# Rotation tables a layer early, joins spread over the blocks, two phase planes and a later turn in a two-model kernel

## The chip, the cores and the metric

The kernel runs on one core of a Trainium2 chip. The metric is the device time of one execution in microseconds (us), the median of several runs. PE is the matrix engine, DVE the vector engine, ACT the scalar engine, POOL is GpSimd, SP the engine that only issues DMAs.

## The reference

Two models run one after the other on one sequence of 256 rows with 1024 features, in float32.

```python
def first_block(x, mem, ...):
    for l in range(2):
        h = rmsnorm(x, g[0])
        y = even_mixer(...) if l % 2 == 0 else odd_mixer(...)   # pooling + gated recurrence / banded attention
        x = x + rmsnorm(y, g[1])
        x = x + rmsnorm(memory_cross_attention(rmsnorm(x, g[2]), mem_n, ...), g[3])
        x = x + rmsnorm(squared_relu_mlp(rmsnorm(x, g[4]), w_ff1[l], w_ff2[l]), g[5])

def second_block(x, ...):
    h = x + diff_attention(rms_norm(x, n0), w_qkv, q_gain, k_gain, lam_vecs, subln, w_o, lam, cos, sin)
    h = h + squared_relu_mlp_2(rms_norm(h, m0), w_up[0], w_down[0])
    h = h + s5_layer(rms_norm(h, n1), a, log_dt, b, c, d_skip, w_glu)     # diagonal state space, both directions
    return h + squared_relu_mlp_2(rms_norm(h, m1), w_up[1], w_down[1])
```

`diff_attention` normalizes each head of q and k, multiplies by a gain and rotates the head by `cos` and `sin`; its two softmax maps are subtracted with a factor made from `lam_vecs`. `s5_layer` is a linear recurrence over 256 steps in 64 groups of 16 features.

## The kernel before, in words

**Layout.** The running value `X` lies as two row tiles of 128 rows (t = 0 and 1). Each float32 operand of a matmul is held as two reduced-precision parts (hi and lo), so every product is three matmuls. A weight comes by a 512 KB load on SP's queue into `raw` (four buffers); ACT rounds it into `whi` (L53, L47), DVE makes `wlo` (L58, L49). Ten `whi` and ten `wlo` tiles form a ring.

**Order.** A list scheduler puts the instructions of each engine in order. Every engine and every DMA queue then works in that order. `manual_schedule(engines=...)` keeps the order of the code for some engines, `low(...)` lowers the priority of what is made inside it.

**Residual.** `residual(t, acc, ...)` normalizes a projection's result and adds it to `X`: DVE `y` (L187), ACT square, DVE `r` (L170), POOL power (L171), DVE `r` (L194) and two `X` (L200). Then PE turns the row tile (tp, L140), and ACT and DVE (L144) make its hi and lo features for the next projection. `row_scale(t)` makes the row factor of the next norm by the same square, `r` and power; the square is ACT's `junk<-X` (L168).

**End of the first model.** At the start of its second MLP, `reorder` writes `X` to DRAM (`d_x`) and reads it back in another row order. That MLP (`perm`) needs `row_scale` of the reordered `X` only at its end, for the residual. Next comes `diff`, which loads cos, sin, the gains and `lam_vecs` and makes the rotation tables (L661 to L674: 17 small DVE operations, one ACT exponential) before the q and k projections.

**Tables of the state-space layer.** While the second MLP of the first model and the first MLP of the second run, the generator `tables` fills in work for blocks 0 to 7 and 8 to 15. Per block POOL makes complex products (`cmt`, L1165 and L1166) that DVE's `gr` and `er` use, and POOL issues DMAs of `gr`, `eo` and `kl` to DRAM (`d_g`, `d_e`, `d_kl`). After the eighth block of a half, POOL joins the eight `kl` of the half in DRAM (two DMAs d_ks<-d_kl, L1450 and L1451), and then issues eight DMAs d_tt<-d_ks (L1456) that re-lay them. The layer loads `e`, `t` (from `d_tt`) and `g` on SP's queue.

**State-space layer.** `ssm` begins when the MLP's residual is done: 48 scaled copies `xp` (L1522 on DVE, L1524 on ACT, L1526 on POOL; two loops over t, the first over both halves h at once, the second half by half), then PE turns them (utp, L1538), multiplies with `e` (zt), rotates phases with the planes of `tbs` (cos, sin, minus sin; two buffers), and makes the outputs from `t` and `g` (yp). `h` (L1610, L1611) are DVE's products with the planes.

**Even mixer.** Its last step normalizes the recurrence's output `y` (L1124), PE turns it (otp, L1127), ACT and DVE make features from it, and the projection `w_out` follows.

## Time and profile before

| | |
|---|---|
| three runs, median (lowest to highest) | 1492.5 us (1489.15 to 1496.48) |
| the profiled execution | 1488.93 us, span of its core 1487.2 us |
| PE busy | 1414.7 us, 95% of the span |
| DVE, ACT, POOL busy | 1103.8, 859.4, 234.4 us |
| mean granted clock of PE | 0.985 of full speed |

PE is busy nearly all the time, so what it waits for is the difference between its 1414.7 us and the span: some 72 us in all, in places that the view of waits names. A change of another engine's work counts where such a place hangs on it.

### The profile page before, as it was taken

How to read it: one execution, taken by the hardware profiler on the slowest of the kernel's cores; microseconds unless marked ns; L12 is line 12 of the kernel's file. 1: busy time of each engine (PE TensorE's matmuls, PEld its weight loads, DVE VectorE, ACT ScalarE, POOL GpSimd, SP SyncE). 2: the span in 40 equal slices, each digit the busy share in tenths (PEclk: the TensorE clock that was granted, in tenths of full speed). 3: DMA queues.
4: the chain of work that ended last, by engine and by line, in shares of the span. 5: the costliest groups of instructions: out<-in, count | busy, mean ns of one | idle time of the engine just before them, and what ended most of it. 6: DMA issues, size and time to landing. Idle time of an engine off the chain costs nothing.

```text
span 1487.2 us, 25549 instructions
## 1 busy us (share of the span) xinstructions
PE 1414.7 (95%) x9668; PEld 1231.5 (83%) x9668; DVE 1103.8 (74%) x1965; ACT 859.4 (58%) x1480; POOL 234.4 (16%) x290
## 2 busy tenths in 40 slices
PE   8899999999999999999999789999999878999997
PEld 8897888998889798878888667888889666889895
DVE  7996658997676866569998589889995487665651
ACT  7475547565564665566656557667656463554540
POOL 1232001000010000014634210033551200000000
PEclk9999999999999999999999999999999998999999
DMA  8465535475875356366677734357779977455640
GB/s 302 143 198 170 185 125 177 157 257 193 287 256 184 119 180 200 112 207 207 220 242 265 254 124 142 100 161 241 238 236 334 346 280 262 153 187 180 210 159 29
DMA packets 121236, 298.26 MB, mean 201 GB/s; under 512 B 15129, under 2 KB 24121, under 8 KB 120473
## 3 DMA queue, kind: packets, MB, share of 16 engines
q1 hardware_dynamic: 113848, 271.40, 55.3%
q0 software_dynamic: 7264, 25.24, 4.6%
q8 instruction: 76, 1.25, 0.3%
q14 instruction: 48, 0.39, 0.1%
HBM read 270.15 MB, written 31.62 MB: 203 GB/s over the span
## 4 chain that ended last, share of the span: by engine, by line
PE 73%; DVE 13%; DMA 6%; issue 4%; ACT 3%; POOL 1%; SPq 0%; DVEq 0%; ACTq 0%; POOLq 0%
PE ffacc L217 7%; PE ffacc L219 7%; PE ffacc L218 7%; PE ffps L224 5%; PE ffps L226 5%; PE ffps L225 5%; PE pacc L219 4%; PE pacc L218 4%; PE pacc L217 4%; DVE wlo L58 3%; PE pb L225 3%; PE pb L224 3%; PE pb L226 3%; DMA raw<-in_w_ff 2%; PE ffps L219 2%
## 5 line engine op out<-in xcount | busy, mean ns | idle before, releaser
L58 DVE SCALAR_TENSOR_TENSOR wlo<-raw,gcols,whi 128x512 fp32r<-128x512 f32 (+1 forms) x456 | 356.7, 826 | 75.6 <-ACT whi L53 75.3
L53 ACT ACTIVATE whi<-raw,gcols 128x512 fp32r<-128x512 f32 (+1 forms) x456 | 317.0, 745 | 104.4 <-PE pb L226 17.3
L47 ACT ACTIVATE whi<-raw 128x1024 fp32r<-128x1024 f32 x176 | 182.8, 1055 | 155.6 <-DMA raw<-in_w_ff 59.3
L49 DVE TENSOR_TENSOR wlo<-raw,whi 128x1024 fp32r<-128x1024 f32 x172 | 210.1, 1241 | 84.1 <-ACT whi L47 80.1
L224 PE MATMUL ffps<-hh,whi 128*128 128x256 f32 x768 | 220.2, 287 | 2.7 <-ACT eo L1419 1.5
L226 PE MATMUL ffps<-hl,whi 128*128 128x256 f32 x768 | 218.2, 284 | 0.0
L225 PE MATMUL ffps<-hh,wlo 128*128 128x256 f32 x768 | 217.6, 283 | 0.0
L217 PE MATMUL ffacc<-whi,ah 128*128 128x512 f32 x512 | 204.7, 400 | 0.0
L219 PE MATMUL ffacc<-whi,al 128*128 128x512 f32 x512 | 202.2, 395 | 0.0
L218 PE MATMUL ffacc<-wlo,ah 128*128 128x512 f32 x512 | 202.1, 395 | 0.0
L224 PEld LDWEIGHTS ffps<-hh,whi 128*128 128x128 f32 x768 | 146.0, 190 | 5.3 <-ACT eo L1419 2.0
L225 PEld LDWEIGHTS ffps<-hh,wlo 128*128 128x128 f32 x768 | 145.7, 190 | 0.6
L226 PEld LDWEIGHTS ffps<-hl,whi 128*128 128x128 f32 x768 | 145.8, 190 | 0.0
L219 PEld LDWEIGHTS ffacc<-whi,al 128*128 128x128 f32 x512 | 96.4, 188 | 22.7
L217 PEld LDWEIGHTS ffacc<-whi,ah 128*128 128x128 f32 x512 | 96.5, 188 | 22.5 <-issue 1.8
L218 PEld LDWEIGHTS ffacc<-wlo,ah 128*128 128x128 f32 x512 | 96.5, 189 | 20.8
L225 PE MATMUL pb<-hh,wlo 128*128 128x256 f32 x352 | 101.2, 289 | 2.6 <-DVE wlo L58 2.6
L224 PE MATMUL pb<-hh,whi 128*128 128x256 f32 x352 | 101.2, 290 | 2.2 <-ACT whi L53 2.2
L226 PE MATMUL pb<-hl,whi 128*128 128x256 f32 x352 | 100.8, 287 | 0.0
L171 POOL TENSOR_TENSOR r<-r,mhalf 128x1 f32<-128x1 f32 x32 | 23.3, 730 | 463.9 <-DVE r L170 457.4
L303 ACT ACTIVATE relu<-ffps 128x512 f32<-128x512 f32 x64 | 43.8, 685 | 54.9 <-PE ffps L226 36.4
L225 PEld LDWEIGHTS pb<-hh,wlo 128*128 128x128 f32 x352 | 68.4, 195 | 3.4 <-DVE wlo L58 3.3
(488 smaller groups left out, 3024.9 us busy)
## 6 DMA issues: line engine op xcount, KB each, us to landing
raw<-in_w_ff SPq DMA_DIRECT2D x128, 512.0 KB, 4.6
raw<-in_ffn_w_up SPq DMA_DIRECT2D x64, 512.0 KB, 4.7
raw<-in_ffn_w_down SPq DMA_DIRECT2D x64, 512.0 KB, 4.6
raw<-in_w_mem_kv SPq DMA_DIRECT2D x32, 512.0 KB, 4.7
raw<-in_w_qkv SPq DMA_DIRECT2D x24, 512.0 KB, 4.7
raw<-in_attn_w_qkv SPq DMA_DIRECT2D x24, 512.0 KB, 5.0
raw<-in_w_in_ab SPq DMA_DIRECT2D x20, 512.0 KB, 6.5
raw<-in_w_mem_q SPq DMA_DIRECT2D x16, 512.0 KB, 4.6
```

The lines of the kernel that those rows point to most:

```text
L47: nc.scalar.activation(out=hi, in_=src, func=AF.Copy)
L49: eng.tensor_tensor(out=lo, in0=src, in1=hi.bitcast(F32), op=ALU.subtract)
L53: nc.scalar.activation(out=hi[:, a], in_=src[:, a], func=AF.Copy, scale=g)
L58: nc.vector.scalar_tensor_tensor(out=lo[:, a], in0=src[:, a], scalar=g, in1=hi[:, a].bitcast(F32), op0=ALU.mult, op1=ALU.subtract)
L171: nc.gpsimd.tensor_tensor(out=r, in0=r, in1=self.mhalf[:, 0:1], op=ALU.pow)
L217: nc.tensor.matmul(o, xh, wh[:, s], start=first, stop=False)
L218: nc.tensor.matmul(o, xh, wl[:, s], start=False, stop=False)
L219: nc.tensor.matmul(o, xl, wh[:, s], start=False, stop=last)
L224: nc.tensor.matmul(out, wh, xh, start=first, stop=False)
L225: nc.tensor.matmul(out, wl, xh, start=False, stop=False)
L226: nc.tensor.matmul(out, wh, xl, start=False, stop=last)
L303: nc.scalar.activation(out=o, in_=ps if view is None else ps.rearrange("p (f c j) -> p f c j", f=2, j=8), func=AF.Relu)
```

## The change

1. The rotation tables move from `diff` to a method `rotations`, called ahead of the MLP that stands before `diff`, with low priority and buffers of their own.
2. `row_scale` of the reordered rows is pinned on ACT behind the output of chunk 3 of that MLP.
3. The joins are made block by block: `join(k - 1)` is issued on POOL's queue in block k. Only the eighth block's join and the eight re-layouts (`step_tables`) come after a half. Those of the first half are pinned on POOL behind the first `prep` of `diff`, those of the second half behind POOL's `xp`; `d_tt` is two tensors.
4. The phase planes are two, not three: minus sin is made by a factor (`nsgn`, or -1.0), and `h1` is two operations. `tbs` has three buffers. POOL's order around `xp` is that of the code.
5. The even mixer's last step for t = 0 and 1 is queued as `features` and taken inside the projection `w_out` (at row tile 1, k tile 2 at the latest); `y` of t = 1 gets a buffer of its own.

```diff
@@ mlp: scales, and the loop over chunks
             for t in range(2):
-                if perm:
-                    self.row_scale(t)
...
-            parts[ch] = out_b(ps)
+            if perm and ch == 3:
+                with self.tc.manual_schedule(engines={nc.scalar.engine}):
+                    parts[ch] = out_b(ps)
+                    for t in range(2):
+                        self.row_scale(t)
+            else:
+                parts[ch] = out_b(ps)
@@ diff
-    def diff(self, pool, w_qkv, gain, q_gain, k_gain, lam_vecs, subln, w_o, cos2, sin2, done):
+    def rotations(self, pool, q_gain, k_gain, lam_vecs, subln, cos2, sin2):
...
-        def rotations():
+        with self.low(600):
...
+        self.tabs, self.sg, self.nlam = tabs, sg, nlam
+
+    def diff(self, pool, w_qkv, gain, w_o, done):
...
-        rotations()
...
-        k0 = prep(0, a, "k", put_k[0])
+        with self.tc.manual_schedule(engines={nc.gpsimd.engine}):
+            k0 = prep(0, a, "k", put_k[0])
+            self.step_tables(0)
@@ even
-            y = self.sb.tile([128, 4, 128], F32, tag="y", name="y")
+            y = pool.tile([128, 4, 128], F32, tag="t2", name="y") if t else self.sb.tile([128, 4, 128], F32, tag="y", name="y")
...
+            self.later.append(features)
+        self.proj_a(hh, hl, w_out, 0, done, turns=HALF, share=True, now=(1, 2))
@@ tables
-                    tb = pool.tile([128, 3, 16, 32], F32, tag="pre_tb", name="tb")
+                    tb = pool.tile([128, 2, 16, 32], F32, tag="pre_tb", name="tb")
-                    V.tensor_scalar(out=tb[:, 2], in0=s1, scalar1=sgn, scalar2=-1.0, op0=MU, op1=MU)
...
+                    if g2 == 0 and k > blocks[0]:
+                        self.join(k - 1)
...
-            nc.gpsimd.dma_start(out=ks[a0:a1, :, :, 112:240], in_=kl5[a0:a1, :, 0, :, 0:128])
-            nc.gpsimd.dma_start(out=ks[a0:a1, :, :, 0:112], in_=kl5[a0:a1, :, 1, :, 32:144])
-            for r in range(8):
-                nc.gpsimd.dma_start(out=self.d_tt[r * 16:r * 16 + 16, 4 * a0:4 * a1, :], in_=src)
+    def join(self, k):
+        self.nc.gpsimd.dma_start(out=ks[:, :, 112:240], in_=kl[:, 0, :, 0:128])
+        self.nc.gpsimd.dma_start(out=ks[:, :, 0:112], in_=kl[:, 1, :, 32:144])
+    def step_tables(self, half):
+        self.join(8 * half + 7)
+        for r in range(8):
+            self.nc.gpsimd.dma_start(out=self.d_tt[half][r * 16:r * 16 + 16], in_=src)
@@ load_phases, ssm
-        t = self.pre.tile([128, 3, 16, 32], F32, tag="tbs", name="tbs", bufs=2)
+        t = self.pre.tile([128, 2, 16, 32], F32, tag="tbs", name="tbs", bufs=3)
...
+        with self.tc.manual_schedule(engines={G.engine}):
+            for t in range(2):
...
+            self.step_tables(1)
...
-            V.tensor_tensor(out=h1, in0=sr, in1=tbs[:, 1:3], op=MU)
+            V.tensor_tensor(out=h1[:, 0], in0=sr[:, 0], in1=tbs[:, 1], op=MU)
+            V.scalar_tensor_tensor(out=h1[:, 1], in0=sr[:, 1], scalar=-1.0, in1=tbs[:, 1], op0=MU, op1=MU)
@@ first model, layer 1
+        if l == 1:
+            c.rotations(c.rot_pool.__enter__(), ...)
```

Line numbers in the rows below are those of each kernel's own file; in the changed one the rotations are L664 to L677, DVE's `xp` is L1544, `cmt` is L1178 and L1179, the joins are L1467 and L1468, d_tt is L1475, d_g is L1420, d_e is L1432 and d_kl is L1448.

The first place is DVE at the end of the first model's second MLP, where ffacc_7392 and ffacc_7393 (before) hold the MLP's result for row tile 0, and 7394 and 7395 that for row tile 1. Before:

```order
L187 TENSOR_TENSOR y<-ffacc_7392,gB 128x512
L187 TENSOR_TENSOR y<-ffacc_7393,gB 128x512
L170 TENSOR_SCALAR r<-ms 128x1
L58 SCALAR_TENSOR_TENSOR wlo<-raw,gcols,whi 128x512 x16
L661 TENSOR_SCALAR qkg<-qkg 128x64
...
L669 TENSOR_TENSOR lp<-lv 128x128
L671 TENSOR_REDUCE ls<-lp 128x2
L673 TENSOR_TENSOR nlam<-ls 128x1
L674 TENSOR_SCALAR nlam<-nlam 128x1
L194 TENSOR_TENSOR r<-r,rsq 128x1
L200 SCALAR_TENSOR_TENSOR X<-y,r,X 128x512 x2
L187 TENSOR_TENSOR y<-ffacc_7394,gB 128x512
```

The same place in the changed kernel, where 7430 and 7431 are row tile 0 and 7432 and 7433 row tile 1:

```order
L187 TENSOR_TENSOR y<-ffacc_7430,gB 128x512
L187 TENSOR_TENSOR y<-ffacc_7431,gB 128x512
L170 TENSOR_SCALAR r<-ms 128x1
L194 TENSOR_TENSOR r<-r,rsq 128x1
L200 SCALAR_TENSOR_TENSOR X<-y,r,X 128x512 x2
L58 SCALAR_TENSOR_TENSOR wlo<-raw,gcols,whi 128x512 x3
L170 TENSOR_SCALAR r<-ms 128x1
L58 SCALAR_TENSOR_TENSOR wlo<-raw,gcols,whi 128x512 x3
L144 TENSOR_TENSOR hl<-tp,hh 128x512 x2
L58 SCALAR_TENSOR_TENSOR wlo<-raw,gcols,whi 128x512 x4
L187 TENSOR_TENSOR y<-ffacc_7432,gB 128x512
L187 TENSOR_TENSOR y<-ffacc_7433,gB 128x512
```

The residual of row tile 0 (L194, L200) now stands right behind its L170; sixteen `wlo` and the tables stood between. On PE the eight turns `tp` of row tile 0 stood behind the last matmul of the MLP; before:

```order
L217 MATMUL ffacc_7395<-whi,ah 128x512
L218 MATMUL ffacc_7395<-wlo,ah 128x512
L219 MATMUL ffacc_7395<-whi,al 128x512
L140 MATMUL tp<-ident,X 128x128 x8
L217 MATMUL acc_9369<-whi,hh 128x512
```

In the changed kernel they stand 24 matmuls ahead of the MLP's end, in this piece:

```order
L217 MATMUL ffacc_7433<-whi,ah 128x512
L218 MATMUL ffacc_7433<-wlo,ah 128x512
L219 MATMUL ffacc_7433<-whi,al 128x512
L140 MATMUL tp<-ident,X 128x128 x8
L217 MATMUL ffacc_7432<-whi,ah 128x512
```

So the MLP's last 24 matmuls, and then 21 of the next projection (`acc`), now stand between the turns of row tile 0 and the first of row tile 1.

The second place is DVE at the start of the state-space layer, where ffacc_11129 to 11132 (before) hold the MLP's result, two tiles for each row tile. Before:

```order
L200 SCALAR_TENSOR_TENSOR X<-ffacc_11129,rsq,X 128x512
L200 SCALAR_TENSOR_TENSOR X<-ffacc_11130,rsq,X 128x512
L170 TENSOR_SCALAR r<-ms 128x1
L49 TENSOR_TENSOR wlo<-raw,whi 128x1024 x2
L200 SCALAR_TENSOR_TENSOR X<-ffacc_11131,rsq,X 128x512
L200 SCALAR_TENSOR_TENSOR X<-ffacc_11132,rsq,X 128x512
L170 TENSOR_SCALAR r<-ms 128x1
L1522 TENSOR_SCALAR xp<-X,r 32x16x16 x11
L1522 TENSOR_SCALAR xp<-X,r 32x8x16 x22
```

In the changed kernel:

```order
L200 SCALAR_TENSOR_TENSOR X<-ffacc_11151,rsq,X 128x512
L170 TENSOR_SCALAR r<-ms 128x1
L1544 TENSOR_SCALAR xp<-X,r 32x16x16 x11
L49 TENSOR_TENSOR wlo<-raw,whi 128x1024 x2
L200 SCALAR_TENSOR_TENSOR X<-ffacc_11152,rsq,X 128x512
L200 SCALAR_TENSOR_TENSOR X<-ffacc_11153,rsq,X 128x512
L1527 TENSOR_SCALAR nsgn<-sgn 128x1
L170 TENSOR_SCALAR r<-ms 128x1
L1544 TENSOR_SCALAR xp<-X,r 32x8x16 x22
```

The eleven copies of row tile 0 stand ahead of the residual of row tile 1. The third place is POOL in the middle of a half, in one block of `tables`; `d_kl` is that block's last DMA. Before:

```order
L1434 DMA d_kl<-kl 128x144
L1408 DMA d_g<-gr 128x1024
L1165 TENSOR_TENSOR cmt<-pk,bb 128x512
L1166 TENSOR_TENSOR cmt_8773<-pk,bb 128x512
L1420 DMA d_e<-eo 128x512 x2
```

In the changed kernel:

```order
L1448 DMA d_kl<-kl 128x144
L1420 DMA d_g<-gr 128x1024
L1467 DMA d_ks<-d_kl 64x1x128
L1468 DMA d_ks<-d_kl 64x1x112
L1432 DMA d_e<-eo 128x512 x2
L1178 TENSOR_TENSOR cmt<-pk,bb 128x512
L1179 TENSOR_TENSOR cmt_8824<-pk,bb 128x512
```

The join, which must wait until `d_kl` has landed, now stands ahead of the products that DVE needs for the next block; this is so, or nearly so, in fourteen blocks.

## Rows read from the trace of the kernel before

**Rows 1.** Waits of PE: waited for, us in total, times, longest.

```profile
PE tp L140 <- issue: 11.1, 1, 11.1
PE utp L1538 <- DVE xp L1522: 9.2, 1, 9.2
...
PE yp L1617 <- DMA g<-d_g: 4.0, 3, 2.1
...
PE fftp L345 <- ACT relu L307: 3.1, 1, 3.1
PE otp L1127 <- DVE y L1124: 2.7, 2, 2.0
```

**Rows 2.** PE's timeline around the MLP's end: start, us, instruction, idle before.

```profile
845.71 0.40 PE L217 MATMUL ffacc<-whi,ah 128*128 128x512 f32 x1
...
846.88 0.40 PE L219 MATMUL ffacc<-whi,al 128*128 128x512 f32 x1
858.36 1.94 PE L140 MATMUL tp<-ident,X 128*128 128x128 f32 x8 [11.09 <-issue]
```

**Rows 3.** DVE's timeline, same place.

```profile
837.69 0.21 DVE L170 TENSOR_SCALAR r<-ms 128x1 f32<-128x1 f32 x1 [0.85 <-ACT junk L168]
...
846.94 5.43 DVE L58 SCALAR_TENSOR_TENSOR wlo<-raw,gcols,whi 128x512 fp32r<-128x512 f32 x8 [3.03 <-ACT whi L53]
853.23 0.20 DVE L661 TENSOR_SCALAR qkg<-qkg 128x64 f32<-128x64 f32 x1 [0.87 <-DMA qkg<-in_attn_q_gain]
...
857.51 1.41 DVE L200 SCALAR_TENSOR_TENSOR X<-y,r,X 128x512 f32<-128x512 f32 x2
858.96 1.29 DVE L187 TENSOR_TENSOR y<-ffacc,gB 128x512 f32<-128x512 f32 x2
...
863.10 1.42 DVE L200 SCALAR_TENSOR_TENSOR X<-y,r,X 128x512 f32<-128x512 f32 x2
```

**Rows 4.** POOL's timeline ahead of it.

```profile
830.73 0.66 POOL L1450 DMA_DIRECT2D d_ks<-d_kl  x1 [5.07 <-DMA d_kl<-kl]
...
834.22 5.09 POOL L1456 DMA_DIRECT2D d_tt<-d_ks  x8 [2.19 <-DMA d_ks<-d_kl]
839.38 0.77 POOL L171 TENSOR_TENSOR r<-r,mhalf 128x1 f32<-128x1 f32 x1
```

**Rows 5.** Windows: us; PE, PEld, DVE, ACT, POOL busy (instructions); PE clock; DMA share; GB/s.

```profile
666.00:671.00 5.00, 4.67 (x27) 4.67 (x28) 5.00 (x6) 3.94 (x7) 3.64 (x3) 0.67 0.64 211
...
700.00:850.00 150.00, 141.94 (x1040) 122.92 (x1038) 125.46 (x186) 93.90 (x156) 65.22 (x78) 1.00 0.75 248
...
858.00:870.00 12.00, 11.64 (x50) 9.51 (x51) 7.20 (x16) 8.11 (x20) 1.65 (x3) 0.82 0.11 40
870.00:940.00 70.00, 65.94 (x344) 53.19 (x343) 67.45 (x150) 46.51 (x89) 6.40 (x3) 1.00 0.45 143
...
1185.00:1197.00 12.00, 4.20 (x59) 3.59 (x62) 10.23 (x34) 7.05 (x17) 4.00 (x9) 0.57 1.03 412
```

**Rows 6.** ACT's timeline where the perm MLP's row factor waits.

```profile
659.70 0.64 ACT L168 ACTIVATE junk<-X 128x512 f32<-128x512 f32 x1 [6.47 <-DMA X<-d_x]
```

**Rows 7.** DVE's timeline at the state-space layer's start, then PE's.

```profile
1182.94 1.45 DVE L200 SCALAR_TENSOR_TENSOR X<-ffacc,rsq,X 128x512 f32<-128x512 f32 x2 [4.90 <-PE ffacc L219]
...
1185.31 10.59 DVE L1522 TENSOR_SCALAR xp<-X,r 32x256 f32<-32x256 f32 x33
...
1192.81 1.94 PE L1538 MATMUL utp<-ident,xp 128*128 128x128 f32 x8 [9.20 <-DVE xp L1522]
```

**Rows 8.** Waits of SP's queue: the loads of the phase planes.

```profile
SPq L1494 <- DVE h L1611: 7.2, 2, 6.5
```

**Rows 9.** One block's product: POOL's timeline, then DVE's.

```profile
789.40 1.39 POOL L1165 TENSOR_TENSOR cmt<-pk,bb 128x512 f32<-128x512 f32 x1 [3.09 <-issue]
...
792.73 0.68 DVE L1169 TENSOR_TENSOR er<-er,cmt 128x512 f32<-128x512 f32 x1
```

**Rows 10.** POOL's groups: busy us, mean ns of one, idle before.

```profile
L1420 POOL DMA_DIRECT2D d_e<-eo x32 | 17.9, 561 | 53.6 <-ACT eo L1419 49.3 <-DVE wlo L49 3.0 <-DMA pk<-d_p 1.3
```

## What the change will do to the time, forecast from the trace

> **What bounds the kernel.** PE works nearly all the time, so I began with the view of what PE waited for [rows 1]. Five of its waits touch the change: 11.1 us for the turns `tp` behind the first model's last MLP, 9.2 us for the turns `utp` of the state-space layer, 4.0 us for `g`, 3.1 us in the reordered MLP and 2.7 us in the even mixer. Next came the timelines around each, to see what ends last there, and then windows, to see which engine binds after it.
>
> The largest is put down to nothing ("issue"). PE's last MLP matmul starts at 846.88 and the turns at 858.36 [rows 2]. DVE's timeline tells why [rows 3]: the residual of row tile 0 had its `r` at 837.69, but in DVE's order sixteen `wlo` (one wait of 3.03 us for ACT among them) and the rotation tables from 853.23 came first, and its two `X` ran at 857.51. POOL's power for it was held too, behind the eight re-layouts, until 839.38 [rows 4]. Afterwards the granted clock averages 0.82 over 858 to 870, a mixture of the lower level (1.2 GHz) just after the idle stretch and the full one, and from 870 to 940 DVE is busy 67.45 of 70 us [rows 5]: there DVE binds, not PE.
>
> **A, the MLP's end.** The tables leave this place and the residual of row tile 0 stands right behind its `r`. The re-layouts are no longer ahead of POOL's power, so with 0.21 for `r`, 0.77 for the power [rows 4], as much as `r` again for the small product and 1.41 for two `X` [rows 3] the row tile is ready at about 837.7 + 2.6 = 840.3. The turns are now placed 24 matmuls before the MLP's end. Matmuls start (846.88 - 845.71) / 5 = 0.234 us apart [rows 2], so that place is at 847.3 - 5.6 = 841.7, and the turns come 1.4 us after their data. The 11.1 us go, and the clock's loss with them, (1 - 0.82) x 12 = 2.2 us [rows 5]: 13.3 us at most. New is the chain of row tile 1. Behind the MLP's last matmul stand 21 matmuls of the projection, 4.9 us. The chain from its `y` to its last `X` took 858.96 to 864.52, 5.6 us [rows 3]; four `wlo` of 0.68 us stand inside it now, in part in its own waits: 5.6 to 8.3 us. PE thus waits 0.7 to 3.4 us; I take 2.0, so A is -11.3 us. The lower bound: if DVE binds from 838 on, only its relief counts, the tables with their waits, from 853.23 to the `X` at 857.51, 4.3 us. I stay near the upper end because DVE is busy only 7.20 of the 12 us from 858 to 870 [rows 5], room for the `wlo` that now come later.
>
> **Where the tables go.** 17 small operations, their six loads and one exponential move into the MLP before, ahead of DVE's first `al`. DVE is not full there, and PE has two chunks in hand: 0.
>
> **B, the row factor.** ACT waited 6.47 us for the reordered `X` [rows 6] with the next chunk's `relu` behind it, and PE waited 3.1 us for that [rows 1], then ran from 666 to 671 at 0.67 of the clock, (1 - 0.67) x 5 = 1.65 us [rows 5]. The factor is used only at the MLP's end. Pinned behind chunk 3 it finds `X` landed: -4.75 at best. In the new order of SP's queue one weight load and the small loads of the first block stand behind the reordered `X`, and DVE's products of these stand ahead of two `wlo`; none is needed before chunk 2 is through, some 20 us later. I take -4.5; bounds 0 and -4.75.
>
> **C, the even mixer.** PE has the projection's matmuls to do while DVE makes `y`; 36 of them are 8.4 us against waits of 2.7 us [rows 1]: -2.5, bounds 0 and -2.7.
>
> **D, the state-space layer's start.** `utp` starts 7.5 us after DVE's first copy; the eleven copies left by then run until 1195.9, 3.1 us [rows 7]. So 22 had to be done. In the new order the eleven large ones of row tile 0 run in the 4.90 us in which DVE waits for PE [rows 7], and eleven small ones, 3.1 us, are left ahead of `utp`: 7.5 - 3.1 = -4.4. A gap of about 4.8 us stays, and so does the low clock (0.57 from 1185 to 1197 [rows 5]). The bound on the other side is 0, if `e`, not `xp`, sets the pace.
>
> **E, planes and the second re-layout.** SP's queue stood 7.2 us for the planes' buffers with loads of `g` behind it [rows 8]; a third buffer ends that. PE's waits for `g` are 4.0 us in all [rows 1], and `g` needs ring slots besides: -1.2, bounds 0 and -4.0. `h1` in two operations adds less than one of 0.68 us [rows 9] in each of four blocks while PE waits for other things: 0, at worst +2.7. Against it, eight re-layouts, 2 MB, move from a stretch where PE never waits into one whose DMA share is already 1.03 [rows 5]. The first half took 8.6 us from join to last issue [rows 4]. Behind POOL's 4.0 us of `xp` [rows 5] this ends near 1185.3 + 4.0 + 8.6 = 1198; the `t` that needs it is loaded later, behind a load that waits for a buffer. What it slows is `e`: I take +1.5, bounds 0 and +6.
>
> **F, the joins.** 28 more DMA issues of 0.66 us [rows 4] are 18 us on POOL, 1.3 us in each of 14 blocks, and each join can wait up to 5.07 us for its `kl` to land [rows 4]. Behind it wait `d_e`, then the next product. DVE takes that product 792.73 - 790.79 = 1.9 us after POOL made it [rows 9]. A join with its wait uses this up; but POOL is busy 65 of 150 us and DVE 125 [rows 5], and `wlo` are made ahead. I take +1.5 us in all, bounds 0 and +14 (1 us a block).
>
> **Sum.** -11.3 - 4.5 - 2.5 - 4.4 - 1.2 + 1.5 + 1.5 = -20.9. The profiled execution took 1488.9 us, so its like would take 1468.0. The median of the runs, 1492.5, is 3.6 above it, so I forecast 1471 (1468.0 + 3.6, rounded down). About 0.5%, 7.5 us, is what a measurement of this kernel can tell from no change: faster is below 1485, slower above 1500.
>
> **Rival 1: DVE takes the place of the wait.** From 870 DVE has 2.5 us to spare in 70 [rows 5]. If the `wlo` that now come later hold the projection back, A gives the 4.3 us of the tables alone, 7.0 less: -13.9, 1479. For it speaks DVE's full stage, against it the idle 4.8 us just ahead. Chance 0.17.
>
> **Rival 2: the second re-layout starves the layer.** If the 2 MB delay `e` and `t` by what they need at the DMA's full load, +6 and the gain of D's 4.4 given back in part (3.0): -20.9 + 4.5 + 3.0 = -13.4, 1479. For it the DMA share of 1.03, against it that the queue keeps this `t` behind everything that is needed earlier. Chance 0.12.
>
> **Rival 3: the joins hold POOL, POOL holds DVE, DVE holds PE.** One mechanism, its place in each of 14 blocks: join ahead of product. A full wait of 5.07 plus 1.3 less the margin of 1.9 is 4.5 us a block, 63 us: -22.4 + 63, 1533. It decides at 7.5 + 22.4 = 29.9 us, 2.1 us a block passed on to PE; from 1.1 us a block on the whole change is within 0.5%, about 1490. Against it: `d_g` often stands between `d_kl` and the join, PE waited for none of these products before, and DVE has slack. Chance 0.05 slower, 0.10 within 0.5%. The longer an issue takes, the likelier this is; a `d_e` issue took 0.561 us on average over 32, all in stretches where DVE was busy [rows 10]. The Trainium skill, "SBUF — State Buffer", in "A bandwidth-pool intuition that's wrong (but worth ruling out)", says that a DMA issued by GpSimd is held while DVE runs a copy in a two-port mode, some 3100 ns instead of 620; by that 28 issues would cost 87 us of POOL, not 18, and this rival would be the likeliest. The 32 issues show no such hold, so its chance stays small.
>
> **Chances and range.** The forecast itself has 0.56 (1464 to 1476, its own range), rivals 1 and 2 have 0.29, also faster; so faster 0.85, within 0.5% 0.10, slower 0.05. The range reaches down to A's and E's best ends without the two costs (-2.0 - 2.8 - 3.0, 1463.6) and some more, 1460, and up through rivals 1 and 2 to 1486.
>
> **What would show it.** A: the turns of row tile 0 lie inside the MLP's matmuls without idle time, row tile 1's wait at most 3.4 us, the clock near full. B: no wait at `fftp`. C: none at `otp`. D: `utp` waits about 4.8 us. E: fewer waits for `g`; `zt` waits more for `e`. F: POOL's wait for `d_kl` in many blocks, but DVE's waits for `cmt` small. Wrong it would be if DVE waits for `cmt` in many blocks, if a `wlo` is late where the tables stood, or if `X` of row tile 0 comes after 841.7 by that clock and stops the MLP itself.

## The result, and the profile after

| | median us (lowest to highest, runs) | profiled execution: time, span |
|---|---|---|
| before | 1490.42 (1488.81 to 1496.48, 5) | 1488.93, 1487.2 |
| after | 1504.56 (1502.31 to 1507.65, 5) | 1503.47, 1501.7 |

The median of before stands here for the five runs beside those of after. The ratio is 1.0091, 95% interval 1.0064 to 1.0119: 14 us slower, where 21 us faster was forecast. No rival gave this time either; the third had the right sign and put it on the joins, but by a mechanism that, as will be seen, the largest wait does not show. One run of f1 was slow (1564.78 us, at a granted clock of 0.842) and is left out of the median of f1 below.

Waits of PE in the profile of after (waited for, us in total, times, longest); the first five answer to [rows 1].

```profile
PE tp L140 <- issue: 1.6, 1, 1.6
PE utp L1561 <- DVE xp L1544: 6.2, 1, 6.2
PE yp L1641 <- DMA g<-d_g: 1.3, 1, 1.3
PE fftp L345 <- ACT relu L307: 1.1, 1, 1.1
PE otp L1138 <- DVE y L1133: 0.5, 1, 0.5
...
PE ffps L224 <- ACT eo L1431: 6.9, 2, 5.9
PE ytp L1664 <- DVE wt L1655: 5.7, 2, 3.9
PE tq L750 <- DVE z L744: 5.4, 2, 3.4
...
PE ffps L225 <- DVE wlo L58: 4.2, 2, 3.5
...
PE ffps L224 <- DVE al L298: 2.1, 1, 2.1
```

All five waits that the prediction aimed at became shorter, by 19.4 us together (11.1 + 9.2 + 4.0 + 3.1 + 2.7 against 10.7), and others took their place. Where, the start times of the same PE instructions tell, read in both traces:

| stretch, by the clock of before | after minus before, us |
|---|---|
| to the reordered MLP (638), with the even mixer (C) | -2.7 |
| 638 to 666, the turns `fftp` (B) | -3.2 |
| 666 to 727 | +6.8 |
| 727 to 847, the MLP's last matmul | +8.5 |
| 847 to 860, the turns behind it (A) | -13.1 |
| 860 to 986, the differential attention | +15.5 |
| 986 to 1181, the next MLP, with the second fill (F) | +2.1 |
| 1181 to 1193, the turns `utp` (D) | -3.0 |
| 1193 to the end (E) | +3.6 |
| sum, as the spans differ | +14.5 |

Each trace is of one execution. At 638 the kernels run below that hold the same edit of the mixer stand between 3.2 us ahead of before and 1.6 us behind it, so a stretch tells differences of 2 or 3 us only where several traces agree.

A went as forecast, which PE's timeline shows where [rows 2] had 11.09 us; the same view has the largest new wait and one in the attention.

```profile
812.55 0.58 PE L224 MATMUL ffps<-hh,whi 128*128 128x256 f32 x1 [5.90 <-ACT eo L1431]
...
863.03 0.63 PE L140 MATMUL tp<-ident,X 128*128 128x128 f32 x4 [1.58 <-issue]
...
944.35 1.97 PE L750 MATMUL tq<-ident,z 128*128 128x128 f32 x8 [3.42 <-DVE z L744]
```

Three places pay for it. **First, the attention.** Windows of after (columns as in [rows 5]):

```profile
858.00:870.00 12.00, 10.35 (x48) 7.90 (x47) 9.11 (x18) 9.66 (x21) 1.54 (x2) 1.00 0.61 192
...
920.00:940.00 20.00, 20.00 (x89) 16.18 (x88) 14.20 (x24) 12.85 (x15) 0.00 (x0) 1.00 0.55 184
940.00:960.00 20.00, 14.74 (x92) 12.33 (x91) 16.84 (x29) 7.42 (x13) 2.06 (x2) 0.83 0.33 106
```

The clock just behind the MLP is full now (1.00 where it was 0.82 [rows 5]), so A's clock term came too. But from 940 to 960 PE is busy 14.74 of 20 us and the clock 0.83: PE has run out of other work. Its order says why. The attention has 288 projection matmuls (`acc`) to put between the turns and scores; how many stand ahead of a group of turns `tq`, or of the second half's scores, was counted in the PE order of each trace:

```
projection matmuls ahead of:             third tq group   second half's first 24 scores
before                                        221                 265
after                                         288                 288
run g1 (below), re-layout not pinned          221                 265
run x2 (below), joins together                211                 288
```

In after all of them are used up before the second key half's `tq`, and nothing is left to cover the chain of turns, scores and softmax behind it. DVE's timeline there:

```profile
937.95 2.69 DVE L58 SCALAR_TENSOR_TENSOR wlo<-raw,sg,whi 128x1024 fp32r<-128x1024 f32 x2 [2.19 <-ACT whi L53]
940.55 1.41 DVE L58 SCALAR_TENSOR_TENSOR wlo<-raw,gcols,whi 128x512 fp32r<-128x512 f32 x2
941.88 1.22 DVE L742 TENSOR_TENSOR z<-z,y 128x1024 f32<-128x1024 f32 x1
...
943.61 1.28 DVE L744 TENSOR_TENSOR z<-z,r 128x512 f32<-128x512 f32 x2
```

And POOL's, with the pinned block of ten issues behind its first `y`:

```profile
874.84 0.68 POOL L1467 DMA_DIRECT2D d_ks<-d_kl  x1
...
878.48 5.00 POOL L1475 DMA_DIRECT2D d_tt<-d_ks  x8 [2.31 <-issue]
897.10 2.39 POOL L739 TENSOR_TENSOR y<-kc,ta 128x1024 f32<-128x1024 f32 x1 [13.63 <-ACT kc L714]
```

POOL is not late: its second `y` is done at 899.5, 42 us before DVE's `z` that uses it (941.88), and POOL waited 13.6 us for ACT ahead of it. DVE was put to the `wlo` of a later weight first, which wait for ACT. The block costs POOL no time; the order that the scheduler drew up around it costs the attention.

**Second, SP's queue at 647.** Timelines of SP's queue, then of DVE, in after:

```profile
647.18 1.28 SPq L1818 DMA_DIRECT2D X<-d_x  x2
648.54 0.42 SPq L42 DMA_DIRECT2D raw<-in_w_ff  x1
649.01 0.42 SPq L1395 DMA_DIRECT2D bc<-in_ssm_bc  x1
649.49 0.42 SPq L1397 DMA_DIRECT2D pk<-d_p  x1
649.95 0.43 SPq L1399 DMA_DIRECT2D gb<-in_ssm_g  x1
...
667.47 0.23 DVE L1178 TENSOR_TENSOR cmt<-bc,pk 128x64 f32<-128x64 f32 x1 [12.01 <-DMA pk<-d_p]
```

DVE stood 12.0 us for `pk`, which was issued at 649.49; POOL's first product, which needs what DVE then makes, ran at 671.46. Behind it in DVE's order stand the `al` and `wlo` for which PE waits 2.1 and 4.2 us (list above). `gb`, 32 KB issued behind `pk`, was as late; the view of DMA issues from 640 to 672 has the us from issue to landing last:

```profile
gb<-in_ssm_g SPq DMA_DIRECT2D x2, 32.0 KB, 17.6
```

The small loads of the first block stand behind the slow read of the reordered `X`. **Third, 812.** ACT's timeline:

```profile
810.96 1.06 ACT L47 ACTIVATE whi<-raw 128x1024 fp32r<-128x1024 f32 x1 [4.91 <-DMA raw<-in_w_ff]
811.92 1.07 ACT L1431 ACTIVATE eo<-etp 128x512 f32<-128x512 f32 x2
```

The eviction `eo` that frees PE's accumulator stands behind a `whi` whose weight lands late (why, below at x2).

### The profile page after: what moved, and what is told of

It reads as the page before. It is cut to its first block, busy times and chain, and to the rows that moved or that the text cites. A ratio compares the mean times of both kernels' runs of the same rounds, so it can differ in the third digit from the quotient of the medians.

```text
span 1501.7 us, 25578 instructions
## 1 busy us (share of the span) xinstructions
PE 1424.2 (95%) x9668; PEld 1236.2 (82%) x9668; DVE 1104.1 (74%) x1966; ACT 861.8 (57%) x1480; POOL 245.7 (16%) x318
## 4 chain that ended last, share of the span: by engine, by line
PE 65%; DVE 15%; DMA 7%; issue 5%; ACT 4%; POOL 3%; SPq 0%; DVEq 0%; ACTq 0%; POOLq 0%
PE ffacc L217 6%; PE ffacc L219 6%; PE ffacc L218 6%; PE ffps L224 5%; PE ffps L226 4%; PE ffps L225 4%; DVE wlo L58 4%; PE pacc L219 3%; PE pacc L217 3%; PE pacc L218 3%; PE pb L224 2%; PE pb L226 2%; PE pb L225 2%; DVE wlo L49 2%; DMA pk<-d_p 2%
## 5 line engine op out<-in xcount | busy, mean ns | idle before, releaser
L53 ACT ACTIVATE whi<-raw,gcols 128x512 fp32r<-128x512 f32 (+1 forms) x456 | 316.9, 745 | 107.6 <-PE pb L226 16.9
L49 DVE TENSOR_TENSOR wlo<-raw,whi 128x1024 fp32r<-128x1024 f32 x172 | 215.2, 1270 | 85.0 <-ACT whi L47 84.4
L217 PEld LDWEIGHTS ffacc<-whi,ah 128*128 128x128 f32 x512 | 96.4, 188 | 22.5 <-issue 1.8
L218 PEld LDWEIGHTS ffacc<-wlo,ah 128*128 128x128 f32 x512 | 96.4, 188 | 20.9
```

The costliest lines, as they stand in the source:

```text
L49: eng.tensor_tensor(out=lo, in0=src, in1=hi.bitcast(F32), op=ALU.subtract)
L53: nc.scalar.activation(out=hi[:, a], in_=src[:, a], func=AF.Copy, scale=g)
L217: nc.tensor.matmul(o, xh, wh[:, s], start=first, stop=False)
L218: nc.tensor.matmul(o, xh, wl[:, s], start=False, stop=False)
```

## The experiments

Every run is compared with runs of the kernel before on the same chip; ratios are to it, with their 95% interval. Runs with the same letter share a chip (z1 shares that of the x runs); between chips the medians of before differ by up to 1.9 us, so across letters the ratios are the better guide. Names: run e1 and so on. The edits, each against the changed kernel:

```
a  first re-layout back at the end of its fill
   -  with manual_schedule(gpsimd): k0 = prep(0, a, "k", put_k[0]); self.step_tables(0)
   +  k0 = prep(0, a, "k", put_k[0])
   +  if blocks[0] == 0: self.step_tables(0)          # last line of ssm_tables
b  first re-layout pinned behind the second rotation:
   +  with manual_schedule(gpsimd): k1 = prep(1, part(D + 512), "k", put_k[1]); self.step_tables(0)
c  first re-layout not pinned:
   +  c.step_tables(0)                                # behind c.diff(...)
d  joins together:
   -  if g2 == 0 and k > blocks[0]: self.join(k - 1)
   +  two dma_start for all 8 blocks, in step_tables
e  table loads:   nc.sync.dma_start(out=cs | sn | gq | gk | sg | lv) -> nc.gpsimd.dma_start
f  read of X:     nc.sync.dma_start(out=c.X[:, t], in_=token_rows(c.d_x, t)) -> nc.gpsimd.dma_start
g  second re-layout back at the end of its fill:  self.step_tables(1) out of ssm, into ssm_tables
h  tables made in the attention, as before:       c.rotations(pool, ...) ahead of c.diff(...)
i  row factor in scales(), as before:             -  manual_schedule(scalar) ... self.row_scale(t)
j  three phase planes with two buffers, as before
```

**Where the first re-layout stands.** e1 has edit a alone.

Expected of e1:

> The changed kernel, but the first half's last join and eight re-layouts are again issued on GpSimd at the end of their fill, ahead of the residual, not pinned behind the first prep. Theory (the place of the re-layouts in GpSimd's order moved the scheduler's plan: with ten DMA issues ahead of the second rotated product y, it put k1's sum, its turns and the scores behind 88 projection matmuls): the order of PE in the attention stage is that of before again, the 14 us lost between 896 and 985 are gone, but GpSimd's power waits for the re-layouts again and sixteen wlo stand ahead of the residual, so PE waits 5 to 8 us for the turns at the MLP's end: 1496 to 1500 us. Rival (the moved tables or the earlier row tiles crowd DVE in the attention stage, whatever the order): the 14 us stay and the MLP's end is lost besides, 1509 to 1514 us.

Measured 1496.81, 1.0040 (1.0025 to 1.0055), as expected: the attention loses 0.9 us instead of 15.5, and A gives 6.4 instead of 13.1. e2 has edit b alone.

Expected of e2:

> The changed kernel, but the first half's last join and re-layouts are pinned on GpSimd behind the second prep (k1) instead of the first (k0). Theory of the plan: the residual at the MLP's end stays early (wait under 3 us), and k1's turns come back into the scores, so most of the 14 us lost in the attention stage return: 1490 to 1494 us. Rival (DVE crowded by earlier data): the stage stays as long as in the changed kernel, 1503 to 1506 us.

Measured 1495.06, 1.0042 (1.0025 to 1.0059). A is kept (-13.1) and the attention loses 6.8: a little more than half of the loss returns, and the time is 1 us above the expected range. Taking the block off POOL's way is right, where it is pinned matters. Four later runs with joins together bear on it: g1 has c, d, e, g; g2 c, d, g, h; g3 b, d, e, g; g4 c, d, e.

Expected of g1:

> The change, but the first re-layout is issued where the scheduler likes, ahead of, between and behind POOL's powers and rotations of the differential attention (not as one pinned block behind the first rotation), the second one at its fill's end as before the change, the joins together, the six table loads on GpSimd's queue. PE's order in the differential attention is then that of the kernel before to the matmul, and the residual of row tile 0 still stands behind two wlo at the MLP's end. Theory (the pinned block cost the attention's plan, not the gain at the MLP's end its worth): about 12 us gained at the turns tp and at most 4 given back in the attention, 1474 to 1481. Rival (DVE is full from there on, so what PE gains at the MLP's end is given back whatever the order): the attention gives 9 to 12 us back, 1485 to 1490.

Expected of g2:

> As the run before it, with the rotation tables made where the kernel before made them, in the attention, instead of a layer ahead. Theory (the gain at the MLP's end hung on the re-layout leaving POOL's queue, not on the tables): the row tile's X is still early, the 17 small operations of the tables (4.3 us with their waits in the profile of before) now stand behind it: 0 to 4 us slower than the run before it, 1475 to 1484. Rival (the tables had to leave as well): the turns tp wait 8 us or more again, 1485 to 1490.

Expected of g3:

> As the first of these four, except that the first re-layout is pinned as one block behind POOL's second rotation y. PE's order in the attention then has the second half's scores 24 matmuls of one projection and 24 of the next later. Theory (the attention's loss is made by the plan that the scheduler draws up around a pinned block of ten issues): 6 to 9 us slower than the first of the four, all of it between the attention's start and its projection's end, 1483 to 1489. Rival (the loss comes from DVE alone): equal to the first of the four within 2 us.

Expected of g4:

> As the first of these four, except that the second re-layout stands in the state-space layer, pinned behind POOL's copies of xp, as in the change. Theory (it starts utp 3 us earlier and delays what the layer loads next by 5): 0 to 4 us slower than the first of the four, 1476 to 1483; utp's wait 6.2 us instead of 9.2, and the 3 us gone again by the layer's end. Rival (the earlier start stays): 3 us faster than the first of the four.

| run | median | ratio | A | attention (860 to 986) | `utp` | 1193 to the end |
|---|---|---|---|---|---|---|
| g1 | 1479.54 | 0.9922 (0.9903 to 0.9941) | -13.1 | +2.1 | 0 | -3.1 |
| g2 | 1480.19 | 0.9925 (0.9910 to 0.9940) | -13.1 | +6.2 | 0 | -1.4 |
| g3 | 1485.06 | 0.9968 (0.9952 to 0.9984) | -13.1 | +11.8 | 0 | -2.1 |
| g4 | 1482.48 | 0.9941 (0.9926 to 0.9957) | -13.1 | +2.5 | -3.0 | +5.2 |

All four lie in the ranges that the theory gave, though g3's 5.5 us behind g1 is just under its 6 to 9. g3 against g1 is the pinned block: 9.7 us more lost in the attention, 5.5 in the medians (in this profile of g3 the MLP ended 5.0 us earlier). g2 against g1: A did not hang on the tables. Made in the attention they go with 4.1 us more there. g1 lost as much more in the MLP (638 to 847), but g3 and g4, with the tables made ahead too, lost only 1.0 and 2.0 more there than g2, so a price of the tables in the MLP is not shown. The medians are 0.65 apart.

**The joins.** x2 has edit d alone.

Expected of x2:

> The change with one edit: the joins are issued two for each half, behind its last block, as before the change, instead of two behind each block's first product. Theory (a join that waits for its lags on POOL holds what stands behind it): the wait of 5.9 us at 812 goes, and 2 to 3 us in the second fill; the attention's order also changes, and loses 7 to 9 us rather than 14: in all 10 to 16 us faster than the change, 1488 to 1495. Rival (the joins cost the 1.5 us of the forecast): 1502 to 1504.

Measured 1488.27, 0.9989 (0.9974 to 1.0005): in the changed kernel the joins alone cost 16 us (15 by the ratios), more than any other part that was taken back by itself. In the traces they are 7.3 of the 8.5 us from 727 to 847, 7.7 of the attention's 15.5 and 2.5 in the second fill. This is no fixed price: the same edit took 4.2 us off e3 (e4 below). They do it by holding POOL only in part, if at all. Its groups in after (busy us, mean ns of one, idle before):

```profile
L1432 POOL DMA_DIRECT2D d_e<-eo x32 | 18.1, 566 | 38.5 <-ACT eo L1431 38.3 <-issue 0.2
L1467 POOL DMA_DIRECT2D d_ks<-d_kl x16 | 10.6, 663 | 17.6 <-DMA d_kl<-kl 16.9 <-issue 0.6
L1468 POOL DMA_DIRECT2D d_ks<-d_kl x16 | 10.3, 643 | 0.2 <-issue 0.2
```

The 32 issues of the joins took 20.9 us with 16.9 of waits for the lags, and POOL still had time to wait 38 us for `eo`. Something of it reaches DVE, whose waits for POOL's `cmt` grew from 1.0 us in before to 7.2 in after (3.9 in x2), in seven pieces of at most 1.3; the largest line of DVE's waits for it in after:

```profile
DVE er L1182 <- POOL cmt L1178: 4.2, 4, 1.3
```

At 812 POOL is not in the chain: DVE's order has changed. In before, after and x2 alike `eo` stands behind the same `whi`. That `whi` needs a weight, and the load of the weight waits until a `wlo` has freed the buffer. Timelines of DVE and SP's queue in after, where the second of two `wlo` has gone behind the products `gr`:

```profile
798.84 1.21 DVE L49 TENSOR_TENSOR wlo<-raw,whi 128x1024 fp32r<-128x1024 f32 x1
...
804.82 4.62 DVE L49 TENSOR_TENSOR wlo<-raw,whi 128x1024 fp32r<-128x1024 f32 x4
...
806.09 0.33 SPq L42 DMA_DIRECT2D raw<-in_w_ff  x1
```

In x2 (DVE, SP's queue, ACT) the two `wlo` stand together, the load is issued 5.1 us sooner and `eo` runs at 807.21, 4.7 us sooner:

```profile
798.60 2.35 DVE L49 TENSOR_TENSOR wlo<-raw,whi 128x1024 fp32r<-128x1024 f32 x2
...
800.98 0.33 SPq L42 DMA_DIRECT2D raw<-in_w_ff  x1
...
806.25 1.06 ACT L47 ACTIVATE whi<-raw 128x1024 fp32r<-128x1024 f32 x1 [0.18 <-PE klag L1442]
807.21 1.07 ACT L1431 ACTIVATE eo<-etp 128x512 f32<-128x512 f32 x2
```

The two `wlo` stand apart in e3 and together in e4 in the same way, and PE's waits for `eo` are 7.0 us in e3 and 0.9 in e4. Why the scheduler parts them when a join stands ahead of the product was not looked into.

**SP's queue.** e3 has b and e, e4 b, d and e.

Expected of e3:

> As the kernel with the re-layouts behind k1, and the six loads of the rotation tables go on GpSimd's queue instead of SP's. Theory: these loads pushed the first block's small loads behind the read of the reordered rows, DVE stood 12 us for pk, and PE lost 6 us between 660 and 720 with it; off SP's queue the first block's bc is loaded early again, DVE's wait for pk falls under 3 us and 5 to 6 us return: 1484 to 1488 us. Rival (the row factor pinned behind chunk 3, or the joins, cost these 6 us): no change from the kernel with the re-layouts behind k1.

Expected of e4:

> As the kernel with the re-layouts behind k1 and the table loads off SP, and the joins of a half are again two DMAs together, issued with the re-layouts. Theory (joins spread over the blocks hold GpSimd and with it DVE and PE: 5.9 us for eo at 812, 2.1 us for er in the second half): 6 to 9 us less than the kernel before it in this list, 1476 to 1481 us. Rival (the wait at 812 is a late weight load, and DVE had slack for the rest): within 2 us of it.

Measured 1496.16, 1.0038 (1.0025 to 1.0051), and 1491.95, 1.0011 (0.9997 to 1.0024). Both missed. Without the table loads PE still waits, 10.3 us in one piece at 670, for `relu`, which stands in ACT's order behind the first block's masks `bm`, which wait for `gb`. In e4 the wait at 812 and the second fill's loss are gone; the attention (+13.3, block still pinned, against +7.4 in e3) and the layer (+6.9 from `utp` on) eat much of the gain, so the edit that took 7.7 us off the attention in x2 goes with 5.9 more there here. So the read itself is the suspect: x1 has f alone, x3 has g1's edits and f.

Expected of x1:

> The change with one edit: the read of the reordered X is issued on GpSimd's queue instead of SP's, so that the small loads of the block and the weights stand behind it in no queue. Theory (these loads were held by a queue that had to finish the slow read first): the small loads land within 5 us of their issue, POOL's wait for pk falls from 12 us to under 5, PE's waits between 666 and 700 (7.4 us in all) go for the most part, 2 to 5 us faster than the change, 1499 to 1503. Rival (the read holds the DMA engines themselves, whatever the queue): the loads land as late as before, 1503 to 1507.

Expected of x3:

> The version with the first re-layout unpinned, the second at its fill's end, the joins together and the table loads on GpSimd's queue (1479.5), and here also the read of the reordered X on GpSimd's queue. Theory (the wait of 11.5 us for the relu there is one for small loads behind that read, but DVE sets the pace of the 100 us behind it, so most of what PE waits less there it waits later): the wait falls below 5 us, and the time by 0 to 4 us, 1475 to 1480. Rival (the wait is worth its length): 6 to 9 us faster, 1470 to 1474.

x1: 1504.23, 1.0088 (1.0067 to 1.0109). The queue theory held (the first small loads land 7 us after their issue, PE is 4.7 us ahead of after at 727), the time did not follow: the rest of the MLP and the attention give all back, and the attention ends at +11.9, as in after (+11.7). x3: 1468.46, 0.9861 (0.9840 to 0.9882). Here my theory that DVE sets the pace fell; at 11 us less than g1 (9 by the ratios) the wait was worth about its length. Views of DMA issues from 640 to 672, of g1:

```profile
bc<-in_ssm_bc SPq DMA_DIRECT2D x2, 128.0 KB, 14.8
pk<-d_p SPq DMA_DIRECT2D x2, 68.0 KB, 14.4
...
gb<-in_ssm_g SPq DMA_DIRECT2D x2, 32.0 KB, 14.6
```

and of x3, where the read is slow still (12.7 us) but holds nothing:

```profile
X<-d_x POOLq DMA_DIRECT2D x2, 512.0 KB, 12.7
...
bc<-in_ssm_bc SPq DMA_DIRECT2D x2, 128.0 KB, 6.8
pk<-d_p SPq DMA_DIRECT2D x3, 68.0 KB, 4.7
...
gb<-in_ssm_g SPq DMA_DIRECT2D x3, 32.0 KB, 6.6
```

In g1 ACT's timeline has the masks' wait ahead of `relu`, and DVE's waits have what `bb` waits for,

```profile
670.81 0.31 ACT L1406 ACTIVATE bm<-bb 128x128 f32<-128x128 f32 x1 [14.88 <-DVE bb L1402]
...
DVE bb L1402 <- DMA gb<-in_ssm_g: 10.6, 1, 10.6
```

and PE's wait for `relu` fell from 11.5 us there to this in x3:

```profile
PE fftp L345 <- ACT relu L307: 1.6, 1, 1.6
```

Which of the two, queue or pinned row factor, releases it? y1 has f alone in the kernel before; y2 is x3 with i.

Expected of y1:

> The kernel before with one edit: the read of the reordered X is issued on GpSimd's queue. Theory (two things hold the relu there, the row factor's wait for X of 6.5 us and, behind it, the small loads; the queue's edit takes away the second alone): PE's wait of 3.1 us at that chunk stays, the products of the blocks come earlier, 0 to 4 us faster than the kernel before, 1486 to 1491. Rival (the queue is the whole cause): 6 us or more faster, below 1484.

Expected of y2:

> The fastest version so far (1468.5: first re-layout unpinned, second at its fill's end, joins together, table loads and the read of X on GpSimd's queue) with one edit taken back: the row factor stands where the kernel before had it, ahead of the next chunk's relu, and waits there for X. Theory (with the queue free, the row factor's wait for X is the last one there and the pin is worth its 4.75 us): PE waits 3 to 6 us there again, 1471 to 1475. Rival (the pin is worth nothing in either case): 1467 to 1470.

y1: 1486.61, 0.9981 (0.9967 to 0.9995), 3 us, though PE's wait at that chunk grew to 7.6 us: ACT now stood 11.1 us for `X`. y2: 1475.39, 0.9905 (0.9887 to 0.9923), 6.9 us behind x3. Both are needed: ACT's timeline of y2 shows the row factor's wait, 8.68 us for the read.

```profile
660.32 0.64 ACT L168 ACTIVATE junk<-X 128x512 f32<-128x512 f32 x1 [8.68 <-DMA X<-d_x]
```

Last, why is the read slow? z1 is g1 (read on SP's queue) with each read split by its outermost size:

```
-  c.nc.sync.dma_start(out=c.X[:, t], in_=token_rows(c.d_x, t))        # sizes 4, 32, 1024
+  for q in range(4):                                                 # 32 rows each
+      c.nc.sync.dma_start(out=c.X[32*q:32*q+32, t], in_=token_rows(c.d_x, 4*t + q))
```

Expected of z1:

> The first version of the fast ones (1479.5: first re-layout unpinned, second at its fill's end, joins together, table loads on GpSimd's queue, read of X on SP's queue) with one edit: each of the two reads of the reordered X, whose source has sizes 4, 32, 1024, is issued as four reads of 32 rows. Theory (the read is slow by its shape, being spread over as few DMA engines as its outermost size gives; the Trainium skill, DMA: Bandwidth & Descriptors, states such a rule, and no row here shows the spread): all eight land within 8 us of the first issue, the small loads behind them in under 8, PE's wait of 11.5 us falls below 4, and the time comes near that with the read on the other queue, 1467 to 1473. Rival (the reordering of rows is slow in any shape): 1477 to 1482.

Measured 1472.46, 0.9882 (0.9862 to 0.9903), 7 us better than g1 (6 by the ratios). Its view of DMA issues:

```profile
X<-d_x SPq DMA_DIRECT2D x8, 128.0 KB, 2.6
...
gb<-in_ssm_g SPq DMA_DIRECT2D x2, 32.0 KB, 2.9
```

SP's timeline has the eight issues:

```profile
649.25 3.96 SPq L1820 DMA_DIRECT2D X<-d_x  x8
```

With 2.6 us to land the same megabyte is there some 6.5 us after the first issue (an estimate from these two lines), and PE does not wait for `relu` at all. Windows of g1 (columns as in [rows 5]) while the two reads hold the queue show what the slow shape does:

```profile
665.00:667.00 2.00, 0.00 (x0) 0.00 (x0) 0.00 (x0) 0.00 (x0) 0.00 (x0) 0.62 0.25 102
667.00:669.00 2.00, 0.00 (x0) 0.00 (x0) 0.00 (x0) 0.00 (x0) 0.00 (x0) 0.50 0.25 101
```

The DMA share, a mean over sixteen engines, is 0.25: as much as four engines busy all the time. The slowness goes with the shape. A split that leaves the outermost size at 4 was not run, so no run of its own tells the shape from the number of reads in flight; that two reads together reach a share of only 0.25 speaks for the shape.

**The layer, and the planes.** f1 keeps the even mixer's turns, the pinned row factor, the order of `xp` and two planes, and takes all moves back (a, d, g, h); f2 is f1 with i; f3 has a, d, h; f4 is f1 with j.

Expected of f1:

> The changed kernel without what it moves for the MLP's end: tables made in the attention stage as before, joins together and both re-layouts at the end of their fills. What stays: the even mixer's later turn, the row factor behind chunk 3, the order of xp, two planes. Theory (the read of the reordered rows holds every load behind it on SP's queue until some 665 us, so the pinned row factor only uncovers the next wait, gb or bc): 3 us from the mixer, 0 to 2 from the row factor, the MLP's end as before (11 us wait): 1484 to 1488 us. Rival (the row factor is worth its 4.5 us where no table loads are in the way, and xp its 4): 1478 to 1481 us.

Expected of f2:

> As the kernel without the moves, and the row factor is not pinned (as before). Theory of the held queue: within 2 us of the kernel with the pin. Rival: 4 to 5 us slower than it.

Expected of f3:

> As the kernel without the moves, but the second half's joins and re-layouts are issued behind xp, inside the state-space layer, as in the changed kernel. Theory (2 MB in a stretch of full DMA delay e and g): 2 to 5 us slower than the kernel without the moves, all of it between the first utp and the last val. Rival (the layer loses elsewhere, by its order or by the planes): within 1 us.

Expected of f4:

> As the kernel without the moves, with three phase planes, two buffers and one h1 operation as before. Theory (a third buffer takes SP's queue waits away and g comes earlier): 1 to 4 us slower than the kernel without the moves. Rival (the two planes changed the order of PE and DVE in the layer to its harm): 1 to 4 us faster.

Measured: f1 1487.05, 0.9975 (0.9959 to 0.9991); f2 1486.88, 0.9971 (0.9956 to 0.9985); f3 1490.28, 0.9992 (0.9976 to 1.0007); f4 1487.73, 0.9972 (0.9954 to 0.9991). f2 shows that the pin alone is worth nothing while the queue is held (PE's wait at `fftp` was 3.8 us without it and 10.5 with it, later chunks level it). f3 against f1 is the second re-layout: `utp` waits 6.2 us instead of 9.2, and from there to the end the layer loses 4.8 where f1 gains 3.2, as g4 against g1; the medians are 3.2 apart. f4 loses that gain (-0.4 against -3.2 in the trace), but f2, with two planes like f1, has -1.2 there and y2 -0.6, and the medians of f1 and f4 do not tell them apart.

## Why the prediction was wrong, step by step

- **A: right in size, wrong about what it hung on and what came behind.** -13.1 against -11.3 forecast. That the re-layouts left POOL's queue is enough for all of it (g2); the tables, which the sum named first, were not needed, and with the re-layouts back 6.4 was left (e1). What failed is the sum's silence on the attention: POOL's ten issues were moved between the two `y` and priced at nothing. They cost POOL nothing indeed. Through the order in which the scheduler then laid the other engines' work they cost PE 5.5 us where they are pinned one rotation later (g3 against g1), and where the change pins them the attention loses 15.5 in the trace, 7.7 of it by the joins (x2). DVE's load, as in rival 1, is not the cause: g1 has the early row tiles and the moved tables too and loses 2.1.
- **F is the largest failed step.** +1.5 forecast, upper bound 14, measured 16 (x2). The mechanism of rival 3 is not what the largest wait shows: POOL waited 16.9 us in all for the lags, DVE 6.2 us longer for POOL's products, and at 812 PE's wait came by DVE's order. An issue took 0.65 us, as [rows 4] let expect; the hold that the Trainium skill states ("SBUF — State Buffer", section "A bandwidth-pool intuition that's wrong (but worth ruling out)") was not seen in these 32 issues, though no trace here tells in which mode DVE ran. How much of the 16 us is POOL's waiting and how much changed order was not separated.
- **B: "none is needed before chunk 2 is through" was wrong.** The prediction named the small loads behind the read on SP's queue; what it had wrong is when they are needed. ACT's masks for the first block wait for them and stand ahead of the next `relu` (g1: 14.88 us, and 11.5 for PE). With the queue free the pin is worth 6.9 us (y2), more than the 4.5.
- **Where the tables go: right in their operations (g2).** Their loads pushed more of the first block's loads behind the read, but with them off SP's queue the time did not fall (e3, 1496.16, against e2, 1495.06).
- **C: right in its mechanism:** the wait at `otp` fell from 2.7 to 0.5 us. That the stretch shows -2.7 against -2.5 is in part luck, since other traces with this edit stand between -3.2 and +1.6 there.
- **D: -3.0 against -4.4,** and the 6.2 us that stay are above the 4.8 forecast. It comes only with the second re-layout in the layer (in g1 and f1 `utp` waits 9.2 as before), and so it is paid for by **E**, for which +1.5 was taken and +6 was the bound: the layer loses 8 us to it in the traces (g4 against g1, f3 against f1), 5 with D's 3.0 taken off, and some 3 us in the medians. The mechanism named, a slower `e`, is not what PE waits for: its waits for `e` were 2.1 us in before and there are none in after and g4, while those for `wt` grew (7.1 us in g4, 4.7 in g1); why was not followed up. Nor did a third buffer end SP's wait for the planes, 6.0 us in after against 7.2. The planes' gain, forecast as 1.2, is 2.8 in one pair of traces and not clear of their scatter.

One sum is off by a little: 1471.6 less 7.8 is 1463.8, not 1463.6, which changes nothing.

What was gained where forecast (A, C, perhaps the planes, and B once the queue is free) makes x3: 1468.46 against the 1490.94 of before beside it, 22.5 us (20.7 by the ratio). That this is close to the sum of 20.9 is luck: x3 lacks D and the second re-layout, and has the read's move, which the change does not have. The change buries its gains under four costs, each of which the sum put at 1.5 us or nothing: joins, pinned block, queue, second re-layout.

## What to carry to other kernels

Where a scheduler orders the engines, a moved or pinned group of instructions is priced twice: by its own time, and by a look at what the order of the *other* engines becomes, above all how much filler PE has left where the next chain of waits begins. Before pinning, try the same edit unpinned (g1 against g3). Prices found this way do not add: the joins cost 16 us in the changed kernel and 4 between e3 and e4. And look up what a slow transfer has behind it in its queue, and when that is needed: splitting or moving one read was worth 6 to 11 us in g1, 3 in the kernel before, and nothing in the changed kernel (x1), where later waits gave it back.

## What the runs showed of the hardware that was not expected

Small loads behind a slow one in the same queue landed 14 to 18 us after their issue (g1, after); with the slow read on GpSimd's queue they took 5 to 7 us (x3). The Trainium skill, "DMA: Bandwidth & Descriptors", in "Rules for kernel authors", says that spreading transfers over issuing engines saves only issue time, since all run on the same DMA engines; here it saved 9 to 11 us (x3 against g1), as loads that stood behind the read no longer waited. The Trainium skill, on the same page, in "Why a DMA increments its semaphore by 16 and not by 1", says that the number of DMA engines over which a transfer is spread is the largest up to 16 that divides the outermost sizes of both its sides. The runs agree: with reads of sizes 4, 32, 1024 holding the queue the DMA share was 0.25 (g1), as much as four of sixteen engines; such a read landed after 12.7 us (x3; 9.3 in y2 and 20.1 in x1), four reads of 32 rows of the same bytes after 2.6 us each (z1), and a weight load of as many bytes after 4.6.
